# Order of the three products of a split weight: all with the high part first, those with the rounding rest last in every chunk

## The chip, the cores and the metric

The kernel runs on one core of a Trainium2 chip. The metric is the device time of one execution in microseconds (us), as the median of several runs. The core has five engines that run their own instruction streams in order: TensorE (PE in the profile, with PEld for the loading of the stationary operand), VectorE (DVE), ScalarE (ACT), GpSimd (POOL) and SyncE (SP, which here issues DMAs).

## The reference

One layer of a streaming encoder on 512 tokens of width 1024, all in float32. First a token mixer: a modulated layer norm, one wide input projection, three branches (a pooling mixer, a latent attention with 8 heads, a spatial gating unit), each projected and weighted with a gate, and an output projection. Then a gated MLP of width 2816 with a causal convolution of three taps. Each half ends with a residual and a layer norm.

```python
h = _modulate(x, sh_t, sc_t)
p = h @ w_in                                 # gates, pool, latents, u and v
y_a = _pool_mixer(a, w_pool, s_pool) @ w_branch[0]
y_b = _mla(cq, ckv, kr, ...) @ w_branch[1]
y_c = _sgu(uv, g_sg, b_sg, w_s, b_s) @ w_branch[2]
merged = gates[:, :, 0] * y_a + gates[:, :, 1] * y_b + gates[:, :, 2] * y_c
x = _layer_norm(ALPHA * x + gt_t * (merged @ w_o)) * ln_t_g + ln_t_b
h = _modulate(x, sh_f, sc_f)
z = conv3(h @ w_up)                          # causal, 3 taps
val, gate = split(z)
x = _layer_norm(ALPHA * x + gt_f * ((silu(gate) * val) @ w_down)) * ln_f_g + ln_f_b
```

## The kernel before

**Products of split numbers.** TensorE multiplies in a rounded format (F32R). To keep float32 accuracy every operand is split into a high part, its rounded value, and a low part, the rest: `a = ah + al`. A product then is three products into one PSUM bank: high with low, low with high, high with high. The helper `mm3` (lines 103 to 106) issues them. In the profile, line 104 is its first product, `wh` with `xl`, line 105 is `wl` with `xh`, line 106 `wh` with `xh`. The first operand of a product is the stationary one; the profile writes "out<-moving,stationary".

**Weight chunks.** Weights come in chunks of 128 x 1024. `wsplit` (lines 86 to 95) loads a chunk into a raw buffer (three in the ring), ACT casts it to the high part (L90), and DVE subtracts that from the raw chunk to make the low part (L91). High and low parts have two buffers each (tags `whi` and `wlo`), shared by all stages. A chunk serves 24 products: 8 blocks of 128 by three, or in `uv_half` and `project_out` 4 token tiles by two by three.

**The stages** in order, with the names that the profile uses:

- first columns and latents, then attention, head by head, with gates (`pg`) between its parts
- pooling (`pool`, out `pa`) and the first merge (`py`) in turn; both take their chunks from a list, `plan`, through `chunk`, which splits one chunk ahead
- the gate row `gtt`: `ada_piece` adds up a modulation from streamed weights on DVE, placed behind the newest split by `behind_split`; `ada_rows` multiplies it out (out `pgt`)
- `uv_half`: v in two halves, then u in two halves; here the token tiles are stationary and the weights move, and four PSUM banks fill side by side
- the second and third merge, with gates between
- `project_out` for the output projection (chunks `o`, out `pyo`): the weights move. POOL multiplies each raw chunk by the gate row (L1003), then ACT casts (L1007) and DVE subtracts (L1008). The first two of eight chunks run through all eight banks one after the other; the last six are resident (L1014, L1015) and finish the banks tile by tile
- residual, layer norm and second modulation, in which the first chunks of the up projection are split ahead (`early`)
- the up projection (`pzu`, chunks `wup`): 44 chunks, six of them early; after each one the convolution on ACT and DVE (L1252 to L1259), the activation, POOL's product (L1270) and the split of the result (L1273, L1274)
- `project_out` for the down projection (chunks `d`, out `pyd`): 22 chunks, the last four resident
- the final layer norm

**What sets the order.** The kernel is written with a tile framework that tracks dependencies and writes each engine's instruction order when it is built, from an estimate of when things are ready. So the order on an engine is not quite the order in the program: gates, for instance, are mixed with parts of the attention. `tc.issue_after` ties an instruction behind another one on its engine.

Of the kernel before, what the change touches and what calls it, by code (L numbers as in the profile page):

```python
# [15 lines left out]
P = 128  # L16
S = 512
D = 1024
KT = 8
TT = 4  # L20
# [30 lines left out]
def trunk(ctx: ExitStack, tc: tile.TileContext, A, out):  # L51
    nc = tc.nc
# [7 lines left out]
    def ps(name):  # L60
        return pp.tile([P, 512], F32, name=name, tag="ps")
# [16 lines left out]
    def f(ap):  # L78
        return ap.bitcast(F32)
# [23 lines left out]
    def mm3(o, wh, wl, xh, xl, start, stop):  # L103
        nc.tensor.matmul(o, wh, xl, start=start, stop=False)  # L104
        nc.tensor.matmul(o, wl, xh, start=False, stop=False)  # L105
        nc.tensor.matmul(o, wh, xh, start=False, stop=stop)  # L106

    def split_ps(src, hi, lo, col=None):
        if col is None:
            nc.scalar.copy(out=hi, in_=src)  # L110
            nc.vector.tensor_tensor(out=lo, in0=src, in1=f(hi), op=ALU.subtract)
        else:
            nc.scalar.activation(hi, src, AF.Copy, scale=col)
            nc.vector.scalar_tensor_tensor(
                out=lo, in0=src, scalar=col, in1=f(hi), op0=ALU.mult, op1=ALU.subtract
            )
# [229 lines left out]
    def gate(b, m, pg=None):  # L346
        if pg is None:
            gh, gl = chunk(("wg", b * KT + m))
            pg = ps("pg")
            for k in range(KT):  # L350
                c = slice(k * P, (k + 1) * P)
                mm3(pg, gh[:, c], gl[:, c], hT_hi[k], hT_lo[k], k == 0, k == KT - 1)
        th = act_t(f"th{b}{m}", F32)
        nc.scalar.activation(th, pg, AF.Tanh, scale=0.5)  # L354
        return th
# [3 lines left out]
    def merge(b, m, bh, bl, th):  # L359
        yh, yl = chunk(("wb", b * KT + m))  # L360
        py = ps("py")
        for k in range(KT):
            c = slice(k * P, (k + 1) * P)
            mm3(py, yh[:, c], yl[:, c], bh[k], bl[k], k == 0, k == KT - 1)
        if b == 0:
            merged[m] = m_t(f"mg{m}")
            nc.vector.scalar_tensor_tensor(
                out=merged[m], in0=th, scalar=1.0, in1=py, op0=ALU.add, op1=ALU.mult
            )
        else:  # L370
            nc.vector.scalar_tensor_tensor(  # L371
                out=th, in0=th, scalar=1.0, in1=py, op0=ALU.add, op1=ALU.mult
            )
            nc.gpsimd.tensor_tensor(out=merged[m], in0=merged[m], in1=th, op=ALU.add)  # L374
# [4 lines left out]
    hT_hi = []  # L379
    hT_lo = []  # L380
# [380 lines left out]
    def pool(m):  # L761
        ah, al = chunk(("wa", m))
        pa = ps("pa")
        for k in range(KT):
            c = slice(k * P, (k + 1) * P)
            mm3(pa, ah[:, c], al[:, c], hT_hi[k], hT_lo[k], k == 0, k == KT - 1)
        g = m // 2
        w = 2 << g
        a = pad_t("apad")
        nc.gpsimd.memset(a[:, 0:16], 0.0)  # L770
        nc.scalar.copy(out=a[:, 16:528], in_=pa)
        cur, lo_ = a, 0
        for lev in range(g + 1):
            sh = 1 << lev
            nx = pad_t("asum")
            nc.gpsimd.tensor_tensor(  # L776
                out=nx[:, lo_ + sh : 528], in0=cur[:, lo_ + sh : 528],
                in1=cur[:, lo_ : 528 - sh], op=ALU.add,
            )
            cur, lo_ = nx, lo_ + sh  # L780
        edge = sm.tile([P, 16], F32, name="edge", tag="edge")
        nc.vector.tensor_tensor(
            out=edge[:, : w - 1], in0=cur[:, 16 : 16 + w - 1],
            in1=kst[:, K_CNT + 16 * g : K_CNT + 16 * g + w - 1], op=ALU.mult,
        )
        nc.vector.tensor_tensor(
            out=edge[:, : w - 1], in0=edge[:, : w - 1], in1=a[:, 16 : 16 + w - 1], op=ALU.subtract
        )
        nc.vector.scalar_tensor_tensor(
            out=cur[:, 16:528], in0=cur[:, 16:528], scalar=1.0 / w, in1=a[:, 16:528],  # L790
            op0=ALU.mult, op1=ALU.subtract,
        )
# [20 lines left out]
    for g in range(4):  # L813
        if g % 2 == 0:
            wh, wl = chunk(("wpool", g // 2))
        for mo in range(2):
            m = 2 * g + mo
            pm = ps("pmx")
            for k in range(2):
                o = (g % 2) * 512 + k * 256 + mo * P  # L820
                c = slice(o, o + P)
                mm3(pm, wh[:, c], wl[:, c], po_hi[2 * g + k], po_lo[2 * g + k], k == 0, k == 1)
            xh = act_t(f"mx{m}h")
            xl = act_t(f"mx{m}l")
# [5 lines left out]
    def uv_half(i, nm, hook=None):  # L830
        tiles = [act_t(f"{nm}{i}{t}", F32) for t in range(TT)]
        pu = [ps("pu") for _ in range(TT)]
        for q in range(4):
            wh, wl = chunk(("wsg", i, q))
            for t in range(TT):
                ts_ = slice(t * P, (t + 1) * P)
                for kk in range(2):
                    k = 2 * q + kk
                    c = slice(kk * 512, (kk + 1) * 512)
                    mm3(pu[t], hT_hi[k][:, ts_], hT_lo[k][:, ts_], wh[:, c], wl[:, c], k == 0, k == KT - 1)  # L840
            if hook:
                hook(q)
        for t in range(TT):
            nc.scalar.activation(tiles[t], pu[t], AF.Gelu)
        return tiles
# [172 lines left out]
    def project_out(src, nk, resident, left_hi, left_lo, gt, dst, chain, name):  # L1018
        acc = [[ps("py" + name) for _ in range(2)] for _ in range(TT)]

        def step(t, n, k, w):
            ts_ = slice(t * P, (t + 1) * P)
            mm3(acc[t][n], left_hi[k][:, ts_], left_lo[k][:, ts_], w[0][n], w[1][n], k == 0, k == nk - 1)

        for k in range(nk - resident):
            w = scaled_chunk(src(k), gt, name)
            for t in range(TT):
                for n in range(2):
                    step(t, n, k, w)
        ws = {k: scaled_chunk(src(k), gt, f"{name}{k}", dst) for k in range(nk - resident, nk)}  # L1030
        for t in range(TT):
            for n in range(2):
                for k in range(nk - resident, nk):
                    step(t, n, k, ws[k])
            chain(t, acc[t])

    x1 = [[None, None] for _ in range(TT)]
    h2_hi = [h_t(f"h2T{j}h") for j in range(KT)]
    h2_lo = [h_t(f"h2T{j}l") for j in range(KT)]
# [195 lines left out]
    for i in range(NP):  # L1235
        half = []
        for v in range(2):
            m = 2 * i + v
            if m < NE:
                if v == 0:  # L1240
                    up_early((m, m + 1), 1)
                pz = pzs[m]
            else:
                with after(3) if m < NE + 2 else ExitStack():
                    uh, ul = wsplit(A["wup"][m], D, "wup")
                pz = ps("pzu")
                for k in range(KT):
                    c = slice(k * P, (k + 1) * P)
                    mm3(pz, uh[:, c], ul[:, c], h2_hi[k], h2_lo[k], k == 0, k == KT - 1)
            cc = C_CONV + 4 * m  # L1250
            t = pt_t("zc")
            nc.scalar.activation(  # L1252
                t, pz, AF.Identity, bias=cols[:, cc + 3 : cc + 4], scale=cols[:, cc + 2 : cc + 3]
            )
            nc.vector.scalar_tensor_tensor(  # L1255
                out=t[:, 1:512], in0=pz[:, 0:511], scalar=cols[:, cc + 1 : cc + 2],
                in1=t[:, 1:512], op0=ALU.mult, op1=ALU.add,
            )
            nc.vector.scalar_tensor_tensor(  # L1259
                out=t[:, 2:512], in0=pz[:, 0:510], scalar=cols[:, cc : cc + 1],  # L1260
                in1=t[:, 2:512], op0=ALU.mult, op1=ALU.add,
            )
            half.append(t)
        val, gate = half
        if i % 2 == 1 and i < 2 * KT:
            ada_piece(3, i // 2)
        if i == 2 * KT:
            gt_f = ada_rows(3, 1, "gtf")
        nc.scalar.activation(gate, gate, AF.Silu)  # L1269
        nc.gpsimd.tensor_tensor(out=val, in0=val, in1=gate, op=ALU.mult)  # L1270
        ah = act_t(f"f{i}h")
        al = act_t(f"f{i}l")
        nc.scalar.copy(out=ah, in_=val)  # L1273
        nc.vector.tensor_tensor(out=al, in0=val, in1=f(ah), op=ALU.subtract)  # L1274
        a_hi.append(ah)
        a_lo.append(al)
# [137 lines left out]
```

## Time and profile before

| | us |
|---|---|
| median of 3 runs | 1004.75 (1003.79 to 1005.43) |
| the profiled execution | 1005.82 |
| its span, first to last instruction | 1003.7 |
| PE busy | 965.4 |
| DVE busy | 601.0 |
| ACT busy | 386.6 |
| POOL busy | 301.1 |

A row of a timeline gives the start in us, the duration in us, engine, line, operation and tiles, the shape of the instruction, and in brackets the idle time of the engine before it and what ended that. A row with a count (x2) merges several. A row of the waits view gives who waited for whom, the idle time in total, the count and the longest. Products on PE are pipelined: one is shown as 0.39 us long, but the next starts 0.23 us after it. So for PE the distance between starts tells the pace.

### The profile page before, as it was taken

The numbers are of one execution on the slowest core, as the hardware profiler recorded it, in microseconds if no ns is written. First come the engines' busy times: TensorE is split into PE (matmuls) and PEld (weight loads), VectorE is DVE, ScalarE is ACT, GpSimd is POOL, SyncE is SP. The second block draws the span as 40 slices with busy tenths as digits, with TensorE's granted clock in tenths as the row PEclk, the third lists the DMA queues.
The fourth block names the chain that finished last, engine by engine and source line by source line (L and its number), as shares of the span: only waits on it lengthen the run. The fifth ranks groups of instructions, "written<-read, shape, count | busy, mean of one in ns | idle before, by whom it ended". The sixth has DMA issues, their size and how long they took to land.

```text
span 1003.7 us, 12194 instructions
## 1 busy us (share of the span) xinstructions
PE 965.4 (96%) x4530; PEld 801.5 (80%) x4530; DVE 601.0 (60%) x923; ACT 386.6 (39%) x656; POOL 301.1 (30%) x311
## 2 busy tenths in 40 slices
PE   4999999999999999999999997999999999999996
PEld 3888888878877888888888876998888888788885
DVE  6947655546666565666434477777656675532267
ACT  3555555442323322433232234554434444321221
POOL 3555110212350011200011755421111121566664
PEclk9999999999999999999999998999999999999998
DMA  9713111115444542363222263124333433342322
GB/s 336 267 39 93 48 51 51 57 63 189 148 131 148 191 136 97 105 220 126 75 93 89 92 225 118 42 84 128 125 121 110 126 126 106 91 140 89 101 84 84
DMA packets 45274, 119.18 MB, mean 119 GB/s; under 512 B 5280, under 2 KB 8736, under 8 KB 45216
## 3 DMA queue, kind: packets, MB, share of 16 engines
q1 hardware_dynamic: 44784, 118.25, 36.0%
q8 instruction: 35, 0.57, 0.2%
q10 hardware_dynamic: 432, 0.17, 0.1%
q14 instruction: 23, 0.19, 0.1%
HBM read 116.30 MB, written 2.10 MB: 118 GB/s over the span
## 4 chain that ended last, share of the span: by engine, by line
PE 77%; DVE 6%; DMA 6%; POOL 5%; issue 3%; ACT 2%; SPq 0%; DVEq 0%; POOLq 0%; ACTq 0%
PE pzu L104 7%; PE pzu L106 7%; PE pzu L105 7%; PE pg L105 4%; PE pg L104 4%; PE pg L106 4%; PE pyd L106 4%; PE pyd L105 4%; PE pyd L104 4%; PE py L104 3%; PE py L105 3%; PE py L106 3%; PE pu L105 3%; PE pu L106 3%; PE pu L104 3%
## 5 line engine op out<-in xcount | busy, mean ns | idle before, releaser
L1270 POOL TENSOR_TENSOR zc<-zc 128x512 f32<-128x512 f32 x22 | 32.7, 1484 | 179.1 <-ACT zc L1269 179.1
L1003 POOL TENSOR_TENSOR d<-d,gtfb 128x512 f32<-128x512 f32 x44 | 72.9, 1676 | 42.1 <-DMA d<-in_wdn 39.3
L374 POOL TENSOR_TENSOR mg<-mg,th 128x512 f32<-128x512 f32 x16 | 22.7, 1416 | 150.5 <-DVE th L371 150.5
L1255 DVE SCALAR_TENSOR_TENSOR zc<-pzu,cols,zc 128x511 f32<-128x511 f32 x44 | 32.8, 747 | 50.1 <-ACT zc L1252 49.9
L1252 ACT ACTIVATE zc<-pzu,cols 128x512 f32<-128x512 f32 x44 | 34.2, 779 | 71.2 <-PE pzu L106 71.2
L1008 DVE TENSOR_TENSOR dl<-d,dh 128x1024 fp32r<-128x1024 f32 x18 | 29.0, 1613 | 52.1 <-ACT dh L1007 52.1
L91 DVE TENSOR_TENSOR wgl<-wg,wgh 128x1024 fp32r<-128x1024 f32 x22 | 27.7, 1260 | 48.6 <-ACT wgh L90 47.4
L721 DVE SCALAR_TENSOR_TENSOR ada<-adar,cact,ada 128x512 f32<-128x512 f32 x56 | 54.6, 1015 | 0.1
L90 ACT CAST wbh<-wb 128x1024 fp32r<-128x1024 f32 x24 | 25.2, 1051 | 70.3 <-PE py L106 65.9
L91 DVE TENSOR_TENSOR wbl<-wb,wbh 128x1024 fp32r<-128x1024 f32 x24 | 38.3, 1595 | 18.4 <-ACT wbh L90 18.3
L91 DVE TENSOR_TENSOR wupl<-wup,wuph 128x1024 fp32r<-128x1024 f32 x38 | 46.9, 1234 | 0.0
L1007 ACT CAST dh<-d 128x1024 fp32r<-128x1024 f32 x18 | 18.9, 1050 | 60.7 <-PE pyd L106 60.6
L90 ACT CAST wuph<-wup 128x1024 fp32r<-128x1024 f32 x38 | 39.5, 1039 | 0.0
L91 DVE TENSOR_TENSOR wsgl<-wsg,wsgh 128x1024 fp32r<-128x1024 f32 x16 | 19.6, 1224 | 33.2 <-ACT wsgh L90 33.2
L354 ACT ACTIVATE th<-pg 128x512 f32<-128x512 f32 x22 | 13.1, 597 | 59.5 <-PE pg L106 59.5
L1259 DVE SCALAR_TENSOR_TENSOR zc<-pzu,cols,zc 128x510 f32<-128x510 f32 x44 | 32.7, 747 | 1.3
L90 ACT CAST wsgh<-wsg 128x1024 fp32r<-128x1024 f32 x16 | 16.8, 1050 | 42.8 <-PE pu L106 38.0
L1003 POOL TENSOR_TENSOR o<-o,gttb 128x512 f32<-128x512 f32 x16 | 26.4, 1677 | 19.6 <-DMA o<-in_wo 16.7
L254 DVE SCALAR_TENSOR_TENSOR acc<-ada,cact,acc 128x256 f32<-128x256 f32 x48 | 29.2, 671 | 0.0
L642 POOL TENSOR_SCALAR pe<-pe,mx 128x128 f32<-128x128 f32 (+3 forms) x32 | 16.8, 533 | 35.7 <-DVE mx L641 26.3
L90 ACT CAST wgh<-wg 128x1024 fp32r<-128x1024 f32 x22 | 23.1, 1051 | 10.1 <-PE pu L106 4.7
L776 POOL TENSOR_TENSOR asum<-apad 128x527 f32<-128x527 f32 x8 | 8.5, 1065 | 56.8 <-issue 25.8
(1375 smaller groups left out, 3182.9 us busy)
## 6 DMA issues: line engine op xcount, KB each, us to landing
wup<-in_wup SPq DMA_DIRECT2D x44, 512.0 KB, 3.5
adar<-in_ada SPq DMA_DIRECT2D x64, 256.0 KB, 3.9
wb<-in_wb SPq DMA_DIRECT2D x24, 512.0 KB, 3.5
wg<-in_wg SPq DMA_DIRECT2D x22, 512.0 KB, 3.6
d<-in_wdn SPq DMA_DIRECT2D x22, 512.0 KB, 3.5
ada<-in_ada SPq DMA_DIRECT2D x32, 256.0 KB, 5.0
wsg<-in_wsg SPq DMA_DIRECT2D x16, 512.0 KB, 3.6
wa<-in_wa SPq DMA_DIRECT2D x8, 512.0 KB, 3.6
```

Of the source, the lines that this page charges most:

```text
L90: nc.scalar.copy(out=hi[:, :n], in_=raw[:, :n])
L91: ins = nc.vector.tensor_tensor(out=lo[:, :n], in0=raw[:, :n], in1=f(hi[:, :n]), op=ALU.subtract)
L104: nc.tensor.matmul(o, wh, xl, start=start, stop=False)
L105: nc.tensor.matmul(o, wl, xh, start=False, stop=False)
L106: nc.tensor.matmul(o, wh, xh, start=False, stop=stop)
L254: ins = nc.vector.scalar_tensor_tensor(out=acc[i], in0=src, scalar=cact[:, k : k + 1], in1=acc[i], op0=ALU.mult, op1=ALU.add,)
L721: nc.vector.scalar_tensor_tensor(out=acc[n], in0=src, scalar=cact[:, k : k + 1], in1=acc[n], op0=ALU.mult, op1=ALU.add,)
L1003: nc.gpsimd.tensor_tensor(out=raw[:, c], in0=raw[:, c], in1=gt[n], op=ALU.mult)
L1252: nc.scalar.activation(t, pz, AF.Identity, bias=cols[:, cc + 3 : cc + 4], scale=cols[:, cc + 2 : cc + 3])
L1255: nc.vector.scalar_tensor_tensor(out=t[:, 1:512], in0=pz[:, 0:511], scalar=cols[:, cc + 1 : cc + 2], in1=t[:, 1:512], op0=ALU.mult, op1=AL ...
L1259: nc.vector.scalar_tensor_tensor(out=t[:, 2:512], in0=pz[:, 0:510], scalar=cols[:, cc : cc + 1], in1=t[:, 2:512], op0=ALU.mult, op1=ALU.add,)
L1270: nc.gpsimd.tensor_tensor(out=val, in0=val, in1=gate, op=ALU.mult)
```

## The change

All places where a whole weight chunk is multiplied no longer call `mm3`. A new helper issues a chunk's 16 products with the weight's high part first and its 8 products with the low part last:

```diff
+    def mm_chunk(o, wh, wl, xh, xl):
+        cs = [slice(k * P, (k + 1) * P) for k in range(KT)]
+        for k, c in enumerate(cs):
+            nc.tensor.matmul(o, wh[:, c], xl[k], start=k == 0, stop=False)
+            nc.tensor.matmul(o, wh[:, c], xh[k], start=False, stop=False)
+        for k, c in enumerate(cs):
+            nc.tensor.matmul(o, wl[:, c], xh[k], start=False, stop=k == KT - 1)
```

`gate`, `merge`, `pool` and the up projection's chunks that are not early use it, each in the same way:

```diff
-            for k in range(KT):
-                c = slice(k * P, (k + 1) * P)
-                mm3(pg, gh[:, c], gl[:, c], hT_hi[k], hT_lo[k], k == 0, k == KT - 1)
+            mm_chunk(pg, gh, gl, hT_hi, hT_lo)
```

In `uv_half` and in the chunks of `project_out` that are not resident, the loop over token tiles runs twice per chunk, first with the high part, then with the low part:

```diff
         for q in range(4):
             wh, wl = chunk(("wsg", i, q))
-            for t in range(TT):
-                ...
-                    mm3(pu[t], hT_hi[k][:, ts_], hT_lo[k][:, ts_], wh[:, c], wl[:, c], k == 0, k == KT - 1)
+            for rest in range(2):
+                for t in range(TT):
+                    ...
+                        if rest:
+                            nc.tensor.matmul(pu[t], hh, wl[:, c], start=False, stop=k == KT - 1)
+                        else:
+                            nc.tensor.matmul(pu[t], hl, wh[:, c], start=k == 0, stop=False)
+                            nc.tensor.matmul(pu[t], hh, wh[:, c], start=False, stop=False)
```

```diff
         for k in range(nk - resident):
             w = scaled_chunk(src(k), gt, name)
-            for t in range(TT):
-                for n in range(2):
-                    step(t, n, k, w)
+            for rest in range(2):
+                for t in range(TT):
+                    ...
+                    for n in range(2):
+                        o = acc[t][n]
+                        if rest:
+                            nc.tensor.matmul(o, hh, w[1][n], start=False, stop=False)
+                        else:
+                            nc.tensor.matmul(o, hh, w[0][n], start=k == 0, stop=False)
+                            nc.tensor.matmul(o, hl, w[0][n], start=False, stop=False)
```

The resident chunks, the early chunks of the up projection, the first columns and the products inside attention, the mixing of the pooled groups and the spatial gating keep `mm3` or their own order. The number of products, their operands and their banks stay the same; the order of summation within a bank changes. No load, cast or subtraction is added or removed.

More of the change, by code (lines that the diff above doesn't have):

```diff
@@ L361, in merge @@
         py = ps("py")
-        for k in range(KT):
-            c = slice(k * P, (k + 1) * P)
-            mm3(py, yh[:, c], yl[:, c], bh[k], bl[k], k == 0, k == KT - 1)
+        mm_chunk(py, yh, yl, bh, bl)
         if b == 0:
@@ L763, in pool @@
         pa = ps("pa")
-        for k in range(KT):
-            c = slice(k * P, (k + 1) * P)
-            mm3(pa, ah[:, c], al[:, c], hT_hi[k], hT_lo[k], k == 0, k == KT - 1)
+        mm_chunk(pa, ah, al, hT_hi, hT_lo)
         g = m // 2
@@ L834, in uv_half @@
             wh, wl = chunk(("wsg", i, q))
-            for t in range(TT):
[L836 to L839, printed above, removed]
-                    mm3(pu[t], hT_hi[k][:, ts_], hT_lo[k][:, ts_], wh[:, c], wl[:, c], k == 0, k == KT - 1)
+            for rest in range(2):
+                for t in range(TT):
+                    ts_ = slice(t * P, (t + 1) * P)
+                    for kk in range(2):
+                        k = 2 * q + kk
+                        c = slice(kk * 512, (kk + 1) * 512)
+                        hh, hl = hT_hi[k][:, ts_], hT_lo[k][:, ts_]
+                        if rest:
[3 more added lines that the diff above has]
+                            nc.tensor.matmul(pu[t], hh, wh[:, c], start=False, stop=False)
             if hook:
@@ L1026, in project_out @@
             w = scaled_chunk(src(k), gt, name)
-            for t in range(TT):
-                for n in range(2):
-                    step(t, n, k, w)
+            for rest in range(2):
+                for t in range(TT):
+                    ts_ = slice(t * P, (t + 1) * P)
+                    hh, hl = left_hi[k][:, ts_], left_lo[k][:, ts_]
+                    for n in range(2):
[5 more added lines that the diff above has]
+                            nc.tensor.matmul(o, hl, w[0][n], start=False, stop=False)
         ws = {k: scaled_chunk(src(k), gt, f"{name}{k}", dst) for k in range(nk - resident, nk)}
@@ L1246, in trunk @@
                 pz = ps("pzu")
-                for k in range(KT):
-                    c = slice(k * P, (k + 1) * P)
-                    mm3(pz, uh[:, c], ul[:, c], h2_hi[k], h2_lo[k], k == 0, k == KT - 1)
+                mm_chunk(pz, uh, ul, h2_hi, h2_lo)
             cc = C_CONV + 4 * m
```

## The prediction

> **What bounds the kernel now.** I read the page first (busy shares, the chain), then the PE timeline, then the waits, then the other engines' timelines around the places where PE stood still.
>
> ```profile
> PE 965.4 (96%) x4530; PEld 801.5 (80%) x4530; DVE 601.0 (60%) x923; ACT 386.6 (39%) x656; POOL 301.1 (30%) x311
> PE 77%; DVE 6%; DMA 6%; POOL 5%; issue 3%; ACT 2%; SPq 0%; DVEq 0%; POOLq 0%; ACTq 0%
> ```
>
> PE is the bound: busy for 96% of the span, and 77% of the chain that ended last. The change leaves its 4530 products and 4530 weight loads as they are and only orders them anew. So it can win in two ways alone: by shortening PE's 38 us of idle time (1003.7 - 965.4), or by changing the time from one product to the next. That second time comes from the starts in the PE timeline:
>
> ```profile
> 759.67 0.39 PE L105 MATMUL pzu<-h2T3h,wupl 128*128 128x512 f32 x1
> ...
> 765.11 0.39 PE L105 MATMUL pzu<-h2T3h,wupl 128*128 128x512 f32 x1
> ...
> 559.66 0.39 PE L104 MATMUL py<-sg2l,wbh 128*128 128x512 f32 x1
> ...
> 565.26 0.39 PE L104 MATMUL py<-sg2l,wbh 128*128 128x512 f32 x1
> ...
> 912.64 0.39 PE L104 MATMUL pyd<-dl,f7h 128*128 128x512 f32 x1
> ...
> 913.09 0.39 PE L106 MATMUL pyd<-dh,f7h 128*128 128x512 f32 x1
> 913.33 0.39 PE L104 MATMUL pyd<-dl,f7h 128*128 128x512 f32 x1
> ...
> 918.13 0.39 PE L104 MATMUL pyd<-dl,f8h 128*128 128x512 f32 x1
> ```
>
> Each pair of equal rows lies one chunk of 24 products apart: 5.44 us or 227 ns a product in the up projection, 5.60 us or 233 ns in a merge, 5.49 us or 229 ns in the down projection. Inside a chunk the products run without a break. The step from 913.09 to 913.33 joins two products with the same stationary tile (f7h): at 0.24 us it is no shorter than the others. So bringing products with one stationary tile side by side, as the change does, is priced at nothing.
>
> The waits view, with idle time in total, count and longest, first for PE, then for ACT and DVE:
>
> ```profile
> PE pgt L739 <- POOL adal L734: 1.2, 2, 0.7
> PE pyd L104 <- DVE dl L1008: 1.0, 2, 0.8
> PE pqn L104 <- ACT wqk6h L598: 0.8, 1, 0.8
> PE pyo L104 <- DVE o5l L1015: 0.7, 1, 0.7
> ACT wbh L90 <- PE py L106: 65.9, 17, 5.8
> DVE wbl L91 <- ACT wbh L90: 18.3, 16, 3.6
> ```
>
> Of the subtractions (DVE L91, L1008) that make a low half, only the down projection's dl ever held PE up. Everywhere else a chunk is split long before its turn. The last two rows show what sets the time of a split: ACT waits until PE has let go of the buffer two chunks back, then casts, and only then DVE subtracts.
>
> **The change part by part.**
>
> *Order of the first product.* In `project_out` and `uv_half` the first product of a chunk read the low half. Now 16 of 24 products come before any low half is read, 16 x 0.229 = 3.7 us. The place where this counts is the seam into the down projection:
>
> ```profile
> 870.29 1.04 ACT L1007 CAST dh<-d 128x1024 fp32r<-128x1024 f32 x1
> 872.35 1.22 DVE L1008 TENSOR_TENSOR dl<-d,dh 128x1024 fp32r<-128x1024 f32 x1
> 872.38 0.39 PE L106 MATMUL pzu<-h2T7h,wuph 128*128 128x512 f32 x1
> 873.62 0.51 PE L104 MATMUL pyd<-dl,f0h 128*128 128x512 f32 x1 [0.85 <-DVE dl L1008]
> 881.50 1.05 ACT L1007 CAST dh<-d 128x1024 fp32r<-128x1024 f32 x1
> 884.50 0.40 PE L106 MATMUL pyd<-dh,f1h 128*128 128x512 f32 x1
> 885.06 0.50 PE L104 MATMUL pyd<-dl,f2h 128*128 128x512 f32 x1 [0.16 <-DVE dl L1008]
> ```
>
> PE lost 873.62 - 872.38 - 0.23 = 1.01 us, and two chunks later 885.06 - 884.50 - 0.23 = 0.33 us. The cast of the first chunk was done at 871.33, ahead of PE's 872.61; that of the third at 882.55, where PE would come at 872.61 + 48 x 0.229 = 883.6. The low halves, done at 873.57 and some 885.0, are wanted 3.7 us after those points. So both waits go: 1.3 us. Next late would be the cast, with 1.3 and 1.0 us to spare. Bounds: 1.3, and 0.4 if ACT makes these casts two of their own durations (2.1 us) later.
>
> *When buffers come free.* The high half's last reader moves from the 24th product to the 16th, 8 x 0.227 = 1.8 us earlier. The low half's last reader moves from the 23rd to the 24th (0.2 us later), in `project_out` and `uv_half` from the 22nd (0.5 us). So the cast two chunks on can be done by the time the chunk ends, and the subtraction then starts at the chunk's end instead of one cast (1.05 us) behind it. DVE now waits for PE's last product itself. Behind it on DVE stand the evictions of the same chunk, which wait for that product anyway, and the `ada` pieces placed behind the split; so nobody gets later. The raw buffer, and with it SP's next load, comes free about 1 us sooner. In most stages that buys nothing, since PE waits for none of it. Four places are left where a split lies ahead of one of PE's waits; their gains lie between nothing (the builder's order keeps the path) and the wait or the split's duration.
>
> A, attention:
>
> ```profile
> 172.29 1.05 ACT L90 CAST wgh<-wg 128x1024 fp32r<-128x1024 f32 x1
> 173.37 1.23 DVE L91 TENSOR_TENSOR wgl<-wg,wgh 128x1024 fp32r<-128x1024 f32 x1 [0.36 <-ACT wgh L90]
> 175.06 3.81 SPq L595 DMA_DIRECT2D wqk<-in_wqk  x2
> 179.24 0.50 PE L104 MATMUL pqn<-cT0l,wqk6h 128*128 128x512 f32 x1 [0.78 <-ACT wqk6h L598]
> ```
>
> SP's load of wqk6 stood behind a load that waited for this subtraction. 0 to 0.8 us; I take half, 0.4.
>
> B, the last head:
>
> ```profile
> 201.39 1.04 ACT L90 CAST wah<-wa 128x1024 fp32r<-128x1024 f32 x1
> 202.46 1.23 DVE L91 TENSOR_TENSOR wal<-wa,wah 128x1024 fp32r<-128x1024 f32 x1 [1.70 <-ACT wah L90]
> 208.00 1.11 PE L656 MATMUL ptp<-ident,pe 128*128 128x128 f32 x5 [0.44 <-POOL pe L642]
> ```
>
> DVE stood idle for 1.70 us before this subtraction, and the softmax work of the last head queued behind it. 0 to 1.2 (its duration); I take 0.6.
>
> C, the gate rows:
>
> ```profile
> 291.04 1.31 DVE L91 TENSOR_TENSOR wbl<-wb,wbh 128x1024 fp32r<-128x1024 f32 x1 [1.92 <-ACT wbh L90]
> 297.35 1.23 DVE L91 TENSOR_TENSOR wpooll<-wpool,wpoolh 128x1024 fp32r<-128x1024 f32 x1
> 298.49 1.42 DVE L721 SCALAR_TENSOR_TENSOR ada<-adar,cact,ada 128x512 f32<-128x512 f32 x2
> 301.37 0.50 PE L739 MATMUL pgt<-adal,onesr 128*128 128x512 f32 x1 [0.73 <-POOL adal L734]
> ```
>
> The last `ada` step stands behind the split of wpool, and PE waited 1.2 us for what comes of it. 0 to 1.2; I take 0.6.
>
> D, the output projection's resident chunks:
>
> ```profile
> 548.82 1.23 DVE L91 TENSOR_TENSOR wbl<-wb,wbh 128x1024 fp32r<-128x1024 f32 x1 [3.22 <-ACT wbh L90]
> 553.91 3.50 POOL L1003 TENSOR_TENSOR o<-o,gttb 128x512 f32<-128x512 f32 x2 [10.00 <-DMA o<-in_wo]
> 553.94 2.34 DVE L91 TENSOR_TENSOR wbl<-wb,wbh 128x1024 fp32r<-128x1024 f32 x1 [0.40 <-ACT wbh L90]
> 585.63 9.31 POOL L1003 TENSOR_TENSOR o<-o,gttb 128x512 f32<-128x512 f32 x6 [4.21 <-DMA o<-in_wo]
> ```
>
> These chunks come through a ring of three raw buffers that the merges' subtractions set free, and PE waits for the last of them (0.7 us at o5l alone). The subtraction at 553.94 can gain only its 0.40 us of idle time before it. 0 to 1.1; I take 0.4. The layer-norm stall behind it moves along with it.
>
> The same two subtractions differ, 1.23 us alone and 2.34 us beside POOL's multiplications. [...]
>
> *Evictions of `uv_half`.* Three of the four banks of a half now finish 12, 8 and 4 products later (2.7, 1.8, 0.9 us), so the four Gelus bunch up. Cost nothing: PE goes on in other banks, and no wait of PE on them stands in its waits. If that cover fails, 2.7 us each for four halves at most.
>
> **The sum.** 1.3 + 0.4 + 0.6 + 0.6 + 0.4 = 3.3 us. The profiled execution took 1005.82 us with a span of 1003.7, so 2.1 us lie around it, and stood 1.07 us above the median. 1005.82 - 3.3 = 1002.5; on the median's footing 1004.75 - 3.3 = **1001.4**. With the upper ends, 1.3 + 0.8 + 1.2 + 1.2 + 1.1 = 5.6, it is 999.1; with the lower, 0.4, it is 1004.4.
>
> **The rivals.**
>
> *Only the seam.* The order that the builder writes for ACT and DVE keeps splits where they were, or A to D are taken up by the next wait on the same path. For it: ACT and DVE run in order, and a cast placed behind its chunk's eviction is no earlier than now. Against it: in A and B DVE stood idle for the cast, 0.36 and 1.70 us. 1004.75 - 1.3 = 1003.4.
>
> *A quicker step.* The merges' 233 ns drop to 227 ns when the operands come in another order. Their 3 x 8 x 24 = 576 products would give 576 x 0.0067 = 3.8 us: 997.6. For it: the same products have a different step from stage to stage with nothing else waiting. Against it: the step held through every merge.
>
> *Slower: a longer step.* The up projection's products go from 227 to 233 ns, the step that merges have. The page counts its chunks by their subtractions:
>
> ```profile
> L91 DVE TENSOR_TENSOR wupl<-wup,wuph 128x1024 fp32r<-128x1024 f32 x38 | 46.9, 1234 | 0.0
> ```
>
> Its 38 chunks of 24, 912 products, would cost 912 x 0.0067 = 6.1 us: 1007.5. It makes the kernel slower by over 2 us once some 800 of them step so (3.3 + 2.0 = 5.3 us). For it: a step of 233 ns exists for products of the same shape. Against it: 227 ns held in all of this stage, whatever the other engines did.
>
> *The change does not do what it says.* The order on PE is the builder's, which may mix groups, as gates and attention are mixed today. Then 1004.75.
>
> **How the numbers follow.** Forecast 0.46, only the seam 0.24, quicker step 0.11, longer step 0.14, no effect 0.05. A measurement here tells about 0.2%, 2.0 us, from no change. The forecast and the quicker step are faster by more than that (0.57, and 0.01 of the seam case with a little of A to D); the seam case and no effect lie within it (0.28); the longer step is slower (0.14). The range runs from 998.0, short of the quicker step's end, to 1006.0, part of the way to the longer step: about 2 in 10 are outside.
>
> **What would show it.** Right: no PE wait on dl at the seam, PE's first pyd product right behind the last pzu; casts of a chunk starting 1.8 us before a chunk ends, subtractions at its end; the waits at pgt, wqk6h and o5l smaller. Wrong: a chunk of 24 products that takes other than 5.44, 5.60 and 5.49 us; a PE wait on a high half (dh, wuph); or a new PE wait on v or u tiles.

## The result and the profile after

| | before | after |
|---|---|---|
| median of 6 runs, us | 1004.27 (1002.36 to 1005.43) | 996.75 (995.37 to 998.22) |
| the profiled execution, us | 1005.82 | 998.22 |
| its span, us | 1003.7 | 996.1 |
| PE busy, us | 965.4 | 962.3 |

The ratio is 0.9927, with an interval of 0.9913 to 0.9941: 7.5 us less. The forecast was 1001.4; its range ended at 998.0, 1.25 us above the result. The direction held and so did the mechanism, save in one stretch (D below); the size did not.

The page of the changed kernel, busy times and the chain that ended last:

```profile
PE 962.3 (97%) x4530; PEld 801.6 (80%) x4530; DVE 595.4 (60%) x923; ACT 392.7 (39%) x656; POOL 310.5 (31%) x311
PE 82%; DMA 6%; DVE 5%; POOL 3%; issue 2%; ACT 1%; DVEq 0%; POOLq 0%; SPq 0%; ACTq 0%
```

The same 4530 products; PE's share of the chain went from 77% to 82%, so less of the end hangs on other engines. The span lost 7.6 us and PE's busy time 3.1 (965.4 to 962.3). A part of the latter is that a product behind a wait is shown longer, 0.50 us in place of 0.39, so idle time alone understates what a stall costs. Starts tell it better.

PE's timeline of the changed kernel, pairs of equal rows one chunk apart in the up projection and in a merge:

```profile
856.22 0.39 PE L111 MATMUL pzu<-h2T1l,wuph 128*128 128x512 f32 x1
...
861.66 0.39 PE L111 MATMUL pzu<-h2T1l,wuph 128*128 128x512 f32 x1
...
549.79 0.39 PE L111 MATMUL py<-sg2l,wbh 128*128 128x512 f32 x1
...
555.39 0.40 PE L111 MATMUL py<-sg2l,wbh 128*128 128x512 f32 x1
```

5.44 and 5.60 us, as before. The pace of the products did not change in either direction; all of the gain is waiting that went.

Where it went is read from the starts of the stages. First the rows of the kernel before, then those of the changed one: first product of the rotary queries (`pq`), of pooling (`pa`), of the merges (`py`), of `uv_half` (`pu`), of the output projection (`pyo`), the transposes after its layer norm (`pth`), the up projection's full chunks (`pzu`) and the down projection's resident chunks (`pyd<-d18l`). The rows between them are left out.

```profile
82.46 0.50 PE L104 MATMUL pq<-wqrl,cT0h 128*128 128x512 f32 x1 [0.48 <-ACT cT0h L113]
208.86 0.48 PE L104 MATMUL pa<-hT0l,wah 128*128 128x512 f32 x1
222.91 0.39 PE L104 MATMUL py<-o0l,wbh 128*128 128x512 f32 x1
314.38 0.39 PE L104 MATMUL pu<-wsgl,hT0h 128*128 128x512 f32 x1
569.46 0.40 PE L104 MATMUL pyo<-ol,mgh 128*128 128x512 f32 x1
620.60 0.47 PE L1125 MATMUL pth<-ident,xr 128*128 128x128 f32 x1 [4.56 <-ACT xr L1113]
664.90 0.40 PE L104 MATMUL pzu<-h2T0l,wuph 128*128 128x512 f32 x1
973.07 0.39 PE L104 MATMUL pyd<-d18l,f18h 128*128 128x512 f32 x1
```

```profile
82.47 0.47 PE L104 MATMUL pq<-wqrl,cT0h 128*128 128x512 f32 x1
205.91 0.48 PE L111 MATMUL pa<-hT0l,wah 128*128 128x512 f32 x1
219.95 0.40 PE L111 MATMUL py<-o0l,wbh 128*128 128x512 f32 x1
310.70 0.39 PE L847 MATMUL pu<-wsgh,hT0l 128*128 128x512 f32 x1
565.66 0.40 PE L1044 MATMUL pyo<-oh,mgh 128*128 128x512 f32 x1
614.69 0.48 PE L1141 MATMUL pth<-ident,xr 128*128 128x128 f32 x1 [3.57 <-ACT xr L1129]
658.93 0.40 PE L111 MATMUL pzu<-h2T0l,wuph 128*128 128x512 f32 x1
965.52 0.39 PE L104 MATMUL pyd<-d18l,f18h 128*128 128x512 f32 x1
```

Up to `pq` both took the same time. From there, with the letters of the prediction:

| stretch | before, us | after, us | difference |
|---|---|---|---|
| `pq` to `pa`: A and B | 126.40 | 123.44 | -2.96 |
| `py` to `pu`: C | 91.47 | 90.75 | -0.72 |
| `pyo` to `pth`: D with its layer norm stall | 51.14 | 49.03 | -2.11 |
| `pzu` to `pyd<-d18l`: the seam | 308.17 | 306.59 | -1.58 |
| `pq` to the end of the span | 921.2 | 913.6 | -7.6 |

One execution is one sample, so both kernels were profiled once more (below, with the experiments). The mean of both differences of two: A and B 2.5, C 1.0, D 1.7, seam 1.7, in all 7.0.

The buffers, in four of the page's groups of the changed kernel (count, then busy time and mean ns, then idle time ahead of them and what ended most of it):

```profile
L91 DVE TENSOR_TENSOR wupl<-wup,wuph 128x1024 fp32r<-128x1024 f32 x38 | 48.8, 1285 | 71.4 <-PE pzu L114 45.6
L1016 DVE TENSOR_TENSOR dl<-d,dh 128x1024 fp32r<-128x1024 f32 x18 | 29.7, 1649 | 54.5 <-PE pyd L1042 51.2
L90 ACT CAST wbh<-wb 128x1024 fp32r<-128x1024 f32 x24 | 25.2, 1050 | 71.2 <-PE py L112 54.3
L91 DVE TENSOR_TENSOR wbl<-wb,wbh 128x1024 fp32r<-128x1024 f32 x24 | 31.1, 1294 | 9.9 <-ACT wbh L90 5.5
```

Lines 111 and 112 are now the products with the high part, 114 those with the low part. A cast waits for L112, no longer for a chunk's last product. Most of the waiting of the up and the down projection's subtractions is for PE's L114 or L1042, the low products. The down projection's had waited for the cast, as this row of the page before shows; the up projection's had waited for nothing (0.0 in its row in the prediction), since it stood behind other work of DVE:

```profile
L1008 DVE TENSOR_TENSOR dl<-d,dh 128x1024 fp32r<-128x1024 f32 x18 | 29.0, 1613 | 52.1 <-ACT dh L1007 52.1
```

That is the predicted shift: cast inside the chunk, subtraction at its end.

PE's waits in the changed kernel (idle time in total, count, longest):

```profile
PE pth L1141 <- ACT xr L1129: 4.7, 2, 3.6
...
PE pzu L104 <- DVE h2T2l L1161: 1.9, 1, 1.9
...
PE pgt L743 <- POOL adal L738: 0.8, 1, 0.8
PE pzu L104 <- DVE h2T6l L1161: 0.4, 1, 0.4
...
PE pyo L104 <- DVE o7l L1023: 0.3, 1, 0.3
```

The waits on `dl`, `wqk6h`, `pe` and `o5l` are gone, one of two at `pgt` is left, and the stall behind the output projection's layer norm (`pth`) is shorter by 1.0 us. The wait on h2T2l, 0.8 us before, has grown by 1.1; but the stretch that holds it, `pth` to `pzu`, is 44.24 us against 44.30, so it cost nothing: PE waits there for the same layer norm at another place.

B shows the mechanism in three rows of the changed kernel, ACT's and then DVE's timeline around the last head:

```profile
195.87 1.05 ACT L90 CAST wah<-wa 128x1024 fp32r<-128x1024 f32 x1 [3.34 <-PE pg L112]
199.31 0.60 ACT L360 ACTIVATE th<-pg 128x512 f32<-128x512 f32 x1 [0.77 <-PE pg L114]
```

```profile
199.31 1.23 DVE L91 TENSOR_TENSOR wal<-wa,wah 128x1024 fp32r<-128x1024 f32 x1
```

The cast ran 3.4 us ahead of the chunk's end (199.31 - 195.87; attention's products lie between the gate's), not one cast behind it. The subtraction follows at the chunk's end without the 1.70 us that DVE had stood idle for the cast.

### The profile page after: what moved, and what is told of

Same layout as the page of the kernel before. It is cut to its first block, busy times and chain, and to the rows that moved or that the text cites. A ratio compares the mean times of both kernels' runs of the same rounds, so it can differ in the third digit from the quotient of the medians.

```text
span 996.1 us, 12225 instructions
## 1 busy us (share of the span) xinstructions
PE 962.3 (97%) x4530; PEld 801.6 (80%) x4530; DVE 595.4 (60%) x923; ACT 392.7 (39%) x656; POOL 310.5 (31%) x311
## 4 chain that ended last, share of the span: by engine, by line
PE 82%; DMA 6%; DVE 5%; POOL 3%; issue 2%; ACT 1%; DVEq 0%; POOLq 0%; SPq 0%; ACTq 0%
PE pzu L112 7%; PE pzu L111 7%; PE pzu L114 7%; PE pg L111 4%; PE pg L112 4%; PE pg L114 4%; PE py L111 4%; PE py L114 4%; PE py L112 4%; PE pyd L1045 3%; PE pyd L1042 3%; PE pyd L1044 3%; PE pu L848 3%; PE pu L847 3%; PE pu L845 3%
## 5 line engine op out<-in xcount | busy, mean ns | idle before, releaser
L1011 POOL TENSOR_TENSOR d<-d,gtfb 128x512 f32<-128x512 f32 x44 | 75.3, 1732 | 34.5 <-DMA d<-in_wdn 32.0
L1284 POOL TENSOR_TENSOR zc<-zc 128x512 f32<-128x512 f32 x22 | 29.7, 1349 | 175.4 <-ACT zc L1283 154.6
L378 POOL TENSOR_TENSOR mg<-mg,th 128x512 f32<-128x512 f32 x16 | 31.3, 1959 | 146.0 <-DVE th L375 146.0
L725 DVE SCALAR_TENSOR_TENSOR ada<-adar,cact,ada 128x512 f32<-128x512 f32 x56 | 49.8, 917 | 0.6 <-DMA adar<-in_ada 0.5
L91 DVE TENSOR_TENSOR wbl<-wb,wbh 128x1024 fp32r<-128x1024 f32 x24 | 31.1, 1294 | 9.9 <-ACT wbh L90 5.5
L1283 ACT ACTIVATE zc<-zc 128x512 f32<-128x512 f32 x22 | 13.9, 631 | 42.7 <-DVE zc L1273 42.6
L375 DVE SCALAR_TENSOR_TENSOR th<-th,py 128x512 f32<-128x512 f32 x16 | 11.0, 685 | 32.7 <-PE py L114 32.7
L778 POOL TENSOR_TENSOR asum<-apad 128x527 f32<-128x527 f32 x8 | 12.2, 1522 | 56.7 <-ACT apad L773 29.8
```

What stands on the lines that cost most here:

```text
L91: ins = nc.vector.tensor_tensor(out=lo[:, :n], in0=raw[:, :n], in1=f(hi[:, :n]), op=ALU.subtract)
L725: nc.vector.scalar_tensor_tensor(out=acc[n], in0=src, scalar=cact[:, k : k + 1], in1=acc[n], op0=ALU.mult, op1=ALU.add,)
L1011: nc.gpsimd.tensor_tensor(out=raw[:, c], in0=raw[:, c], in1=gt[n], op=ALU.mult)
```

## The experiments

The theory: **early release of the high buffer**. The cast two chunks on moves off the path, and the stalls that had a split ahead of them shrink. Rivals: the low part is wanted later within its own chunk (a matter of its first reader, not of the buffer); or the products with one stationary tile side by side run better. Each time below is a median beside the median of the kernel before on the same chip, with the ratio's interval.

**The parts alone.** Three kernels, each with the new order in some stages only, nothing else changed.

`project_out`'s loop alone, before its resident chunks:

```diff
+            for rest in range(2):
+                for t in range(TT):
+                    ...
```

> The kernel before, with the new order in project_out's non-resident chunks alone (o 0 and 1, d 0 to 17). Theory (the seam's waits go because the first product no longer needs the low half; the other gains come from the earlier release of the high buffers in gates, merges and pooling): only the seam is gained, 1.6 us, no PE wait on dl L1008, the stretches up to the output projection unchanged; about 1002.7 against 1004.3. Rival (the gain is a chance result of the builder's new order of instructions, whichever stage is touched): no clear split by stage, some other time between 997 and 1005.

1002.91 beside 1005.0, 0.9978 (0.9969 to 0.9987). The seam's waits are gone: `pzu` to `pyd<-d18l` took 306.59 us, as in the changed kernel. A, B and C stayed (126.38 us for `pq` to `pa`).

`mm_chunk` in gates, merges and pooling alone:

```diff
-                mm3(pg, gh[:, c], gl[:, c], hT_hi[k], hT_lo[k], k == 0, k == KT - 1)
+            mm_chunk(pg, gh, gl, hT_hi, hT_lo)
```

> The kernel before, with the new order in gate, merge and pool alone. Theory: the gains up to the end of the layer-norm stall between mixer and MLP are all here, 5 to 6 us (pa starts about 3 us earlier, pgt 3.8, the first full up-projection chunk 6), and PE still waits 1.0 us for dl at the seam into the down projection; about 998.4. Rival (chance order): less than half of that.

998.02 beside 1005.0, 0.9938 (0.9926 to 0.9951): 6.2 us, the larger part. A and B lost 3.01 us, C 0.72, D 2.60 against the kernel before; the seam kept its length (308.13).

The order in `uv_half` and the up projection alone:

```diff
-                    mm3(pz, uh[:, c], ul[:, c], h2_hi[k], h2_lo[k], k == 0, k == KT - 1)
+                mm_chunk(pz, uh, ul, h2_hi, h2_lo)
```

> The kernel before, with the new order in uv_half and in the up projection's chunks alone. Theory: PE waits for no split in these stages, so the time stays within 0.5 us of before, 1004.3; at most the casts and subtractions at the seam come a little earlier. Rival (chance order): a change of over 1 us, either way.

1003.04 beside 1005.0, 0.9986 (0.9976 to 0.9996). The expectation missed: it gained about 1.4 us. The seam's stretch was 306.59 here too, although `project_out` still reads a low part first. DVE's timeline of this kernel shows why, with the subtraction of the down projection's first two chunks:

```profile
863.80 1.92 DVE L1022 TENSOR_TENSOR dl<-d,dh 128x1024 fp32r<-128x1024 f32 x1 [2.77 <-PE pzu L114]
869.24 1.23 DVE L1022 TENSOR_TENSOR dl<-d,dh 128x1024 fp32r<-128x1024 f32 x1 [0.38 <-PE pzu L114]
```

The first low part is ready at 865.72, ahead of PE's first `pyd` product at 868.98, since the up projection's last chunks let the buffers go earlier. So the seam has two causes, either of which is enough, and it is counted once. By their ratios the three parts add up to more than the whole, 2.2 + 6.2 + 1.4 = 9.8 us against 7.3 for all (0.73% of 1004.27). The seam counted twice is 1.6 us of these 2.5; the rest lies within the intervals.

**The high buffer held.** The changed kernel, with one product of `mm_chunk` that reads the high part moved to the chunk's end. The same 24 products, still with 15 high ones first:

```diff
-            nc.tensor.matmul(o, wh[:, c], xh[k], start=False, stop=False)
+            if k < KT - 1:
+                nc.tensor.matmul(o, wh[:, c], xh[k], start=False, stop=False)
         for k, c in enumerate(cs):
-            nc.tensor.matmul(o, wl[:, c], xh[k], start=False, stop=k == KT - 1)
+            nc.tensor.matmul(o, wl[:, c], xh[k], start=False, stop=False)
+        nc.tensor.matmul(o, wh[:, cs[-1]], xh[KT - 1], start=False, stop=True)
```

> The changed kernel, but in mm_chunk one product with the high part (the last block, high with high) is held back to the end of the chunk, so the high buffer comes free as late as before while the low part is still wanted only after 15 products. Theory: the early release of the high buffer is what gains in A to D, so those 5 to 6 us are lost and only the seam's 1.6 us stay; about 1002.5. Rival (the late need of the low half, or the order of products as such, is what gains): the time stays at 996.8.

1003.2 beside 1005.0, 0.9985 (0.9976 to 0.9993). PE's waits in this kernel:

```profile
PE pgt L745 <- POOL adal L740: 1.8, 2, 1.0
...
PE pqn L104 <- ACT wqk6h L604: 0.8, 1, 0.8
...
PE ptp L662 <- POOL pe L648: 0.4, 1, 0.4
```

All three are back, A and B take 126.75 us again, and only the seam's gain stays (`project_out` has the new loop there). One product in the wrong place undoes the change in its largest part. The low parts are still read late here, so it isn't their first reader that matters in A to C, and products with one stationary tile still lie side by side.

**The low buffer freed instead.** The kernel before, with gates, merges and pooling as 8 low products first and 16 high ones last:

```diff
+        for k, c in enumerate(cs):
+            nc.tensor.matmul(o, wl[:, c], xh[k], start=k == 0, stop=False)
+        for k, c in enumerate(cs):
+            nc.tensor.matmul(o, wh[:, c], xl[k], start=False, stop=False)
+            nc.tensor.matmul(o, wh[:, c], xh[k], start=False, stop=k == KT - 1)
```

> The kernel before, with gate, merge and pool multiplying the low part's 8 products first and the high part's 16 last: the low buffer comes free early, the high one as late as before, and the low part is wanted first. Theory (the early release of the high buffer gains, since ACT's cast leads every split): nothing is gained in A to D, and the first product of a chunk may now wait for a subtraction; 1004 to 1006. Rival (any order that frees one of the two buffers early gains, or grouping products by their weight operand as such): as e2, about 998 to 999.

1005.94 beside 1005.38, 1.0004 (0.9995 to 1.0013): no gain. Grouping alone brings nothing, and neither does an earlier low buffer: the split begins with the cast, and the cast needs the high one.

**A third high buffer, old order.** If the buffer is the cause, another buffer should do what the order does. It takes its room from two of 48 activation buffers:

```diff
-        return sb.tile([P, 512], dt, name=name, tag="act", bufs=48)
+        return sb.tile([P, 512], dt, name=name, tag="act", bufs=46)
...
-        hi = wp.tile([P, D], F32R, name=name + "h", tag="whi")
+        hi = wp.tile([P, D], F32R, name=name + "h", tag="whi", bufs=3)
```

> The kernel before in its old order of products, with a third buffer for high parts (two of the 48 activation buffers are given up for its space). Theory (what gains in A to D is that the cast no longer waits for a high buffer): the cast is off the path, the subtraction starts once the low buffer is free, at the end of a chunk, and A to D are gained without any change of order: pa 3 us and pmx 3.7 us earlier, counted from the rotary queries; 998 to 1000 if the two missing activation buffers cost nothing. Rival (the order of the products themselves gains): no gain, 1004 or more.

999.08 beside 1004.19, 0.9941 (0.9919 to 0.9963). Without any change of order A and B lost 1.89 us, some two thirds of the 2.96 that the new order gave, C 0.67 and the seam 1.58. D lost nothing (51.05 us), which the expectation had wrong. This is the strongest run for the theory in A, B, C and the seam, and it says that D, and a part of A and B, have something more in them.

**Gates alone, merges and pooling alone.** The gates first:

> The kernel before, with the new order in gate alone. Theory: A and B (the wait of pqn for wqk6, that before it for wqk4, and the last head's wait for the softmax) are behind splits that wait for a gate's buffer, so pa starts some 3 us earlier counted from the rotary queries, and pgt, the output projection and the seam stay as before; about 1001.5. Rival (the merges' and pooling's release gains at B too): pa only 1.5 us earlier, about 1003.

1001.94 beside 1005.38, 0.9962 (0.9949 to 0.9974). `pq` to `pa` took 123.40 us against 126.40: all of A and B belongs to the gates, whose chunks are mixed with attention. C grew by 2.1 us (last section). The rest:

> The kernel before, with the new order in merge and pool alone. Theory: A and B stay as before (pa within 0.3 us), C gives 0.9 us at pmx, and D 0 to 2 us up to the layer-norm stall; the seam keeps its 1.6 us; about 1002.5. Rival (gates and merges both free buffers for D): C alone, 1003.5.

1002.94 beside 1004.19, 0.9983 (0.9970 to 0.9996). C alone, 0.73 us by its stretch. D was not better (51.33 us), and its stall only changed place; PE's waits in this kernel:

```profile
PE pth L1129 <- ACT xr L1117: 4.9, 3, 3.2
PE pyo L104 <- DVE o5l L1019: 2.3, 2, 2.0
```

The wait at o5l, 0.7 us before, is 2.3 us here, and the stall behind the layer norm 4.9 in place of 5.7.

**Both kernels again**, unchanged, for the scatter of single executions:

> The kernel before once more, for a second trace. Kernels that had nothing changed ahead of the output projection's resident chunks still passed that stretch 0.8 to 0.9 us faster than the first trace of before. If that stretch varies from execution to execution, this trace has it near 45.3 us (first trace 46.2), and D's gain is about 1 us smaller than the first pair of traces says; if not, it has 46.2 again.

> The changed kernel once more, on the chip on which the others run, to compare the version with the resident chunks in the new order (ratio 0.9908 to before): 0.9927 again if that version is truly faster, near 0.991 if the two are equal.

The kernel before took 1003.27 in its one run, and its output projection 44.9 us from the first product to the last, not 46.2: that stretch does vary from trace to trace; the changed one 996.08 beside 1004.19, 0.9920 (0.9901 to 0.9939). The stretches of all traces but the last two below, in us:

| kernel | `pq` to `pa` (A, B) | `py` to `pu` (C) | `pyo` to `pth` (D) | `pzu` to `pyd<-d18l` (seam) |
|---|---|---|---|---|
| before | 126.40 | 91.47 | 51.14 | 308.17 |
| before, again | 125.84 | 92.01 | 50.33 | 308.42 |
| after | 123.44 | 90.75 | 49.03 | 306.59 |
| after, again | 123.71 | 90.74 | 49.00 | 306.59 |
| `project_out` alone | 126.38 | 92.00 | 49.84 | 306.59 |
| `uv_half`, up projection | 126.35 | 91.48 | 50.22 | 306.59 |
| high buffer held | 126.75 | 92.00 | 50.42 | 306.59 |
| low products first | 126.68 | 92.02 | 50.95 | 308.31 |
| gates, merges, pooling | 123.40 | 90.75 | 48.54 | 308.13 |
| gates | 123.40 | 93.57 | 49.96 | 309.01 |
| merges, pooling | 126.08 | 90.74 | 51.33 | 308.75 |
| third high buffer | 124.51 | 90.80 | 51.05 | 306.59 |

The stages A to C and the seam come out within some 0.3 us where the order is the new one. Without it they scatter by up to 0.9 us from trace to trace (C of the gates alone aside, where the clock fell to 0.51 for 3.4 us). D scatters more: it took 49.84 to 51.33 us in all kernels whose gates or merges keep the old order, and 48.40 to 49.35 where both have the new one, the last two runs below included.

**Further in the same direction.** The resident chunks of `project_out` and the early chunks of the up projection kept the old order. The first kernel also puts all low products of the resident chunks last in each bank:

```diff
-                for k in range(nk - resident, nk):
-                    step(t, n, k, ws[k])
+                for k in range(nk - resident, nk):
+                    nc.tensor.matmul(o, left_hi[k][:, ts_], ws[k][0][n], start=False, stop=False)
+                    nc.tensor.matmul(o, left_lo[k][:, ts_], ws[k][0][n], start=False, stop=False)
+                for k in range(nk - resident, nk):
+                    nc.tensor.matmul(o, left_hi[k][:, ts_], ws[k][1][n], start=False, stop=k == nk - 1)
```

> The changed kernel, with the resident chunks of project_out ordered in the same way (for each bank all products with the high parts of its six or four resident chunks first, those with the low parts last). Theory: PE's waits for o5l, o6l and o7l (some 1.1 us in the changed kernel) go, the layer-norm stall stays; 996.0 against 996.8. Rival (those waits are set by POOL's multiplication before the cast, so PE then waits for the high half or idles later): no change, 996.8.

996.49 beside 1005.38, 0.9908 (0.9894 to 0.9922), which cannot be told from the changed kernel's 0.9927 and 0.9920. The wait on o7l (0.3 us) became one on the cast before it, o6h (0.3 us). POOL's multiplications stand ahead of both casts: in the changed kernel ACT waited for them 2.2 us in all before the casts of o6h and 1.1 us before those of o7h, and the order within the resident chunks does not make them earlier.

The second adds the early chunks, with the products of the activations' low part last:

```diff
+        for k in range(KT):
+            for m in ms:
+                ...
+                nc.tensor.matmul(
+                    pzs[m][:, c], uh[k // 4][:, w], h2_lo[k][:, c], start=False, stop=k == KT - 1
+                )
```

> The changed kernel with the resident chunks in that order too, and in the early chunks of the up projection all products with the activations' high part first, those with their low part last. Theory (PE waits 1.9 us for h2T2l and 0.4 us for h2T6l, which DVE makes last): up to 2 us less in addition, about 994.5. Rival (the high half h2T2h comes as late, since the layer norm itself ends late): no change against e6a.

999.66 beside 1005.38, 0.9941 (0.9927 to 0.9954): some 3 us slower than without the second edit. The stretch from `pth` to the first full up chunk holds it: 47.79 us against 45.01. PE's waits in this kernel:

```profile
PE pzu L1243 <- DVE h2T3h L1158: 2.1, 1, 2.1
...
PE pzu L1243 <- DVE h2T7h L1158: 0.9, 1, 0.9
PE pzu L1243 <- ACT h2T6h L1163: 0.8, 1, 0.8
```

Here the parts arrive block by block over k. Going through all k with the high parts first makes PE run into the last block's high part, with two products instead of three per chunk and block to cover the wait. Putting the late operand last helped where a whole chunk is there at once, and hurt here, where the operand itself trickles in. No run was clearly faster than the changed kernel.

## Why the prediction was right in kind and short in size

*The pace of products.* Priced at nothing, and that held (5.44 and 5.60 us). Both rivals with another step fell.

*The seam, 1.3 us.* Right, with its two waits; it came to 1.6 to 1.7. Most of the missing 0.3 is the step behind each wait: from the first product behind the two waits on `dl` in the kernel before to the next one it was 0.35 and 0.34 us instead of 0.23, together 0.2 us more. One thing in it was incomplete: the new order in `project_out` was named as the cause, and the up projection's earlier release is as good a cause by itself.

*When buffers come free.* Right in full: the cast ends inside the chunk, the subtraction begins at its end, and the runs with the buffer held and with a third buffer show that this, and not the later first reader, carries A to C.

*A and B, 0.4 + 0.6 us.* This is one of the two steps that failed: "their gains lie between nothing ... and the wait or the split's duration", with half of it taken. By stretches A gave 1.2 us on the mean of two traces each (`pq` to the last head's first score product: 119.25 and 118.68 before, 117.66 and 117.93 after), B 1.4 (7.15 and 7.16, then 5.78 and 5.78), and each is above its upper bound of 0.8 and 1.2. For A the wait on wqk6 had been priced at its 0.8 us of idle time, but the steps into and out of that product were 1.05 and 0.34 us in place of 0.11 and 0.23 (0.93 and 0.33 in the second trace): 1.0 us on the mean. A smaller wait at 147.5 us, of the same kind for wqk4, is not among PE's waits of that view; it cost 0.4 us in the first trace and is not in the second. For B the bound was the subtraction's 1.23 us; but what moved was the idle time ahead of it, printed in its own row as 1.70 us. The first score product of the last head stood 0.75 us before that subtraction (201.71, 202.46), and now stands 0.82 us after it (200.13, 199.31): 1.57 us.

*C, 0.6 us.* Measured 1.0, inside its bounds. One of the two waits at `pgt` went.

*D, 0.4 us.* The other step that failed: "The subtraction at 553.94 can gain only its 0.40 us of idle time", with a bound of 1.1. Measured 1.7 by the mean, and 1.3 between the nearest traces of the two kernels (50.33 and 49.03). Of it 0.6 lies in the output projection's waits and 1.1 in the layer norm stall. "The layer-norm stall behind it moves along" was wrong: it shrank, because it does not hang on PE's last product. ACT's timeline at the cast of an early up chunk, of the kernel before and of the changed one, shows what it hangs on:

```profile
602.90 1.14 ACT L1059 CAST wuph<-wup 128x512 fp32r<-128x512 f32 x2 [4.50 <-DMA wup<-in_wup]
```

```profile
596.99 1.14 ACT L1075 CAST wuph<-wup 128x512 fp32r<-128x512 f32 x2 [3.94 <-DMA wup<-in_wup]
```

From this cast to the first `pth` it is 17.70 us in both kernels (602.90 to 620.60, 596.99 to 614.69), and so it is in their second traces: on DVE the layer norm's work stands behind the split of this chunk. Counted from the start of `pyo` the cast comes after 33.44 and 32.63 us in the two traces of before, and after 31.33 and 31.30 in those of after. So all of D's gain is there when this chunk's load lands. By the chains of the four traces this load is issued as soon as DVE has split an earlier up chunk and so left a raw buffer: 27.26 and 25.95 us after the start of `pyo` before, 25.51 and 25.15 after. From there it took 6.08 and 6.58 us, then 5.72 and 6.05. On the mean 1.3 us of D are the earlier issue and 0.4 the shorter load. The prediction looked at one subtraction, and not along the raw buffers to this load.

How gates and merges bring the load forward is only partly settled. D came below the scatter of the other kernels (49.84 to 51.33 us) where gates and merges both had the new order, and not with the gates alone (49.96), with merges and pooling alone or with a third high buffer. So D needs the earlier release in both, and the chain of raw buffers, loads and POOL's multiplications ahead of that load was not taken apart. How much of D is whose stays open.

*The sum.* A half of each bound was taken for want of a reason to take more. But A and B were on PE's path, each with DVE idle ahead of it for a cast, and there the whole wait went and more: 2.5 us against the 1.0 of the halves and the 2.0 of the bounds. With C 0.4 above its half, D 1.3 and the seam 0.4, the terms are 1.5 + 0.4 + 1.3 + 0.4 = 3.6 us short; the forecast was 1001.4 - 996.75 = 4.65 too high, and of that 0.5 is the kernel before itself, whose median is 1004.27 over all runs in place of 1004.75. Some 0.6 us stay unassigned.

*Only the seam.* Its condition, that the builder leaves the splits where they were, did not hold: ACT's casts stand ahead of the chunk's eviction now, as in B's rows. The difference between the two subtractions of before (1.23 us alone, 2.34 us beside POOL's multiplications) shows in single rows after as well: in the down projection of the changed kernel the subtraction at 866.90, beside POOL's multiplications from 866.76 on, took 2.23 us, that at 877.88, with POOL idle from 876.05 to 880.90, 1.23. The gains of A to D stood all the same (2.5 us in A and B, 1.0 in C, 1.7 in D).

## What to carry to other kernels

An operand that is split into two buffers need not be freed as a whole: issue the readers of the part that is refilled first ahead of the others, and the refill's first step moves inside the current chunk, which here did at least as much in A to C and the seam as a third buffer. Before pricing such a change, look for every stall that has an idle engine and a cast into that buffer ahead of it, and price the idle time in full, not half, and not the duration of the next instruction. Then follow the buffers that come free to the loads that wait for them, for a stall can hang on one of these. And put the late operand's products last only where a whole chunk waits for it: where blocks arrive one by one, as in the early chunks here, work through each block while it is there.

## What the runs showed of the hardware

The kernel with the new order in the gates alone lost some 1.5 us in C to TensorE's clock. Its PE timeline behind the last wait of the gate rows:

```profile
297.80 0.50 PE L745 MATMUL pgt<-adal,onesr 128*128 128x512 f32 x1 [1.06 <-POOL adal L740]
...
298.63 0.63 PE L105 MATMUL pmx<-po0h,wpooll 128*128 128x512 f32 x1
299.06 0.63 PE L106 MATMUL pmx<-po0h,wpoolh 128*128 128x512 f32 x1
...
302.02 0.39 PE L104 MATMUL pmx<-po1l,wpoolh 128*128 128x512 f32 x1
302.25 0.40 PE L105 MATMUL pmx<-po1h,wpooll 128*128 128x512 f32 x1
```

From 298.63 to 302.02 eight products stepped by 0.42 us instead of 0.23, 8 x 0.19 = 1.5 us. Its windows view has the granted clock in the column after the five engines:

```profile
296.00:298.40 2.40, 1.33 (x5) 0.81 (x6) 2.22 (x3) 0.72 (x1) 1.75 (x1) 1.00 0.04 15
298.60:302.00 3.40, 3.40 (x9) 2.67 (x8) 1.09 (x3) 0.69 (x1) 0.00 (x0) 0.51 0.51 154
302.10:304.00 1.90, 1.90 (x10) 1.54 (x9) 0.74 (x2) 0.69 (x1) 0.00 (x0) 1.00 0.00 0
```

Clock 0.51 for 3.4 us, behind waits of 0.74 and 1.06 us with products between. The second trace of the kernel before had waits of 0.74 and 1.05 us at the same two places, and its clock stayed at 1.00. So of two traces with 1.8 us of waits at these places one lost another 1.5 us at the lower clock and the other nothing; what decides it was not tested.
